# Gate pieces moved into the mixer, the first expert's matrix ahead of the ranking, modulation by token halves, and last rows and statistics ahead of the overflow test

## The chip, the core and the metric

The kernel runs on one core of a Trainium2 chip. The time is device time in microseconds (us) of one execution. Its engines are TensorE (PE; PEld is its weight load), VectorE (DVE), ScalarE (ACT), GpSimd (POOL) and SyncE (SP), which here mainly issues DMAs. Each engine works its own instructions in order and waits on semaphores for the others. All times below are in us from the start of the span unless they are durations.

## The reference

Two decoder layers on 256 tokens of 1024 channels, in float32. Each layer has two sub-layers, a token mixer and a channel mixer, and each sub-layer is modulated by the condition c:

```python
x = layer_norm(x, ln0_g, ln0_b)
for layer in range(DEPTH):
    shift, scale, gate = modulation(c, ada_w[layer, 0], ada_b[layer, 0])
    h = x * (1.0 + scale) + shift
    y = hybrid_mixer(h, ...)          # SSD, latent attention, gMLP, one output projection
    x = layer_norm(DN_ALPHA * x + (1.0 + gate) * y, ...)
    shift, scale, gate = modulation(c, ada_w[layer, 1], ada_b[layer, 1])
    h = x * (1.0 + scale) + shift
    y = swiglu(h, ...) if layer % 2 == 0 else moe_swiglu(h, ...)   # top 2 of 8 experts
    x = layer_norm(DN_ALPHA * x + (1.0 + gate) * y, ...)
```

`modulation` is silu(c) times a 1024x3072 matrix (the "ada" weights), cut into shift, scale and gate. `moe_swiglu` takes the softmax over each token's two best router logits as weights and sums the two experts' outputs.

## The kernel before, in words

The four sub-layers run one after the other: mixer 0, dense, mixer 1, experts. Weights come in chunks of 1 MB (some 0.75 MB) through a ring of buffers; SP issues the DMAs in program order, each as soon as a buffer of the ring is free.

Matmuls that need full precision are made of three (`mm3`, L153 to L155): the weight is split into a rounded part `whi` (ACT, L146) and a rest `wlo` (DVE, L148), the activation into `hhi` and `hlo`, and the products hhi·whi, hlo·whi and hhi·wlo are summed. The experts use a form of it in part, and plain float32 matmuls elsewhere.

A sub-layer starts like this. `residual` (L321, L322) adds the gated output to x, one half of 128 tokens after the other; each half gets its statistics (L285, L289), the power on POOL (L280) and its normalisation on DVE (L325, remembered as `mark["x"]`). `transposed` makes 16 transposes on PE (L332) into four PSUM tiles, each two channel blocks by 256 tokens. `modulated_t` works through these four tiles: scale and shift of one block on ACT (`htmp`, L343), of the other on DVE (L346), then the rounded part of both on ACT (`hhi`, L348), the rest on DVE (`hlo`, L349). Two `htmp` buffers are there. `proj` in the mixer (L153 to L155) and the first pieces of the dense layer then take `hhi` and `hlo` as moving operand, 256 tokens wide, channel block after channel block.

The ada pieces are 24 units of half a shift, scale or gate each: two 1 MB chunks, 16 matmuls (L200), for a gate piece the addition of a bias row on DVE (L223), a copy of the row on ACT (L225), one broadcast matmul on PE (L229, two records in the trace) and the copy into the gate on ACT (L193). `CUT` says which units fall to which stage. Units of a stage are taken from a list wherever "F" stands in `ORDER`, the written order of the steps in a mixer. Those that `CUT` leaves over (`stage[5]`, the two gate pieces of the experts' sub-layer) are worked after mixer 1, held back behind its last normalisation by `issue_after`, which tells the scheduler that an instruction must not be put ahead of another.

Routing (`route`): the normalised x is transposed and copied (`xt`, L812, L814), multiplied with the router (L818), the best two logits are found, `sl` says which expert a token goes to and `pos` at which place (L846). Then the experts are ranked by their counts (`cnt`, L864) on DVE, the ranking's tables are made, and SP loads the experts' numbers. The expert at the first place is known ahead. For each place `gather` makes a selection matrix `hot` (L933) and picks its tokens by matmul (L971, L978). Then the expert's matmuls (L1029, L1037, L1120), and `scatter` (L1165, L1169) adds the result to x. At the end, `overflow` tests whether an expert had more tokens than places (L1206), and works those off; with these inputs it has nothing to do. The last layer norm takes the statistics of x, loads its gain and bias (`lnrow`, L303, a 1 MB broadcast), and finishes four quarters of x on DVE (L1333, L1334) and on ACT with POOL (L1328 to L1330).

## Time and profile before

| | us |
|---|---|
| median of 3 runs | 1257.72 (1256.67 to 1258.25) |
| the profiled execution | 1257.42 |
| its span | 1255.6 |
| TensorE busy | 1170.9 (93%) |
| VectorE busy | 506.3 (40%) |
| ScalarE busy | 384.3 (31%) |
| read from memory | 399.61 MB, 320 GB/s over the span |

In the rows below a line begins with its start and its duration; "x8" says that eight instructions were merged in a row. What stands in square brackets is how long the engine had been idle before, and whose instruction ended the wait. PEclk is the granted clock of TensorE as a share of full speed; the levels are 2.4 GHz (1.00) and 1.2 GHz (0.50).

### The profile page before, as it was taken

The numbers are of one execution on the slowest core, as the hardware profiler recorded it, in microseconds if no ns is written. First come the engines' busy times: TensorE is split into PE (matmuls) and PEld (weight loads), VectorE is DVE, ScalarE is ACT, GpSimd is POOL, SyncE is SP. The second block draws the span as 40 slices with busy tenths as digits, with TensorE's granted clock in tenths as the row PEclk, the third lists the DMA queues.
The fourth block names the chain that finished last, engine by engine and source line by source line (L and its number), as shares of the span: only waits on it lengthen the run. The fifth ranks groups of instructions, "written<-read, shape, count | busy, mean of one in ns | idle before, by whom it ended". The sixth has DMA issues, their size and how long they took to land. (4 is left out here: it accounts for less than half of the span.)

```text
span 1255.6 us, 18705 instructions
## 1 busy us (share of the span) xinstructions
PE 1170.9 (93%) x7667; PEld 704.4 (56%) x7667; DVE 506.3 (40%) x815; ACT 384.3 (31%) x558; POOL 54.5 (4%) x58
## 2 busy tenths in 40 slices
PE   5999979999997999879999999899999999999994
PEld 2877758999986976534433557743334333333331
DVE  2776465777557754521003477630010020300214
ACT  1776435444444754210002457620010010100100
POOL 0100100000000000010000002200000000000001
PEclk9999889999998997989999999999999999999997
DMA  9957646788554475638999999999999999999994
GB/s 378 386 200 295 219 167 227 279 299 332 171 192 167 163 288 198 252 157 312 350 426 408 426 424 367 364 395 349 425 423 371 423 391 426 412 401 375 413 423 163
DMA packets 59592, 402.97 MB, mean 321 GB/s; under 512 B 6751, under 2 KB 7143, under 8 KB 17390
## 3 DMA queue, kind: packets, MB, share of 16 engines
q1 hardware_dynamic: 59358, 401.47, 81.3%
q8 instruction: 62, 1.02, 0.3%
q10 hardware_dynamic: 144, 0.26, 0.1%
q14 instruction: 28, 0.23, 0.0%
HBM read 399.61 MB, written 2.10 MB: 320 GB/s over the span
## 5 line engine op out<-in xcount | busy, mean ns | idle before, releaser
L1029 PE MATMUL mm<-w,xt 128*64 128x512 f32 (+1 forms) x1344 | 288.7, 561 | 0.0
L148 DVE TENSOR_TENSOR wlo<-w,whi 128x1024 fp32r<-128x1024 f32 (+1 forms) x180 | 220.0, 1229 | 111.9 <-ACT whi L146 110.0
L146 ACT ACTIVATE whi<-w 128x1024 fp32r<-128x1024 f32 (+1 forms) x188 | 194.1, 1041 | 177.8 <-PE mm L154 87.8
L1029 PEld LDWEIGHTS mm<-w,xt 128*64 128x64 f32 x1344 | 94.4, 137 | 165.0 <-issue 163.7
L153 PE MATMUL mm<-hhi,whi 128*128 128x256 f32 x608 | 175.5, 290 | 4.8 <-ACT hhi L348 4.8
L154 PE MATMUL mm<-hlo,whi 128*128 128x256 f32 x608 | 174.8, 288 | 0.8 <-DVE hlo L349 0.8
L155 PE MATMUL mm<-hhi,wlo 128*128 128x256 f32 x608 | 173.7, 286 | 0.0
L1072 DVE TENSOR_TENSOR sa<-mm,sa 128x512 f32<-128x512 f32 (+3 forms) x30 | 17.4, 580 | 371.9 <-PE mm L1029 193.0
L1120 PE MATMUL acc<-w,ht 128*64 128x512 f32 x616 | 146.5, 597 | 0.0
L153 PEld LDWEIGHTS mm<-hhi,whi 128*128 128x128 f32 x608 | 118.6, 195 | 9.5 <-ACT hhi L348 6.0
L154 PEld LDWEIGHTS mm<-hlo,whi 128*128 128x128 f32 x608 | 118.6, 195 | 2.4 <-DVE hlo L349 1.8
L155 PEld LDWEIGHTS mm<-hhi,wlo 128*128 128x128 f32 x608 | 118.4, 195 | 0.6 <-issue 0.5
L1120 PEld LDWEIGHTS acc<-w,ht 128*64 128x64 f32 x616 | 43.6, 137 | 81.8 <-issue 80.7
L1071 ACT ACTIVATE sa<-mm 128x512 f32<-128x512 f32 (+3 forms) x30 | 15.2, 507 | 202.6 <-PE mm L1029 116.0
L1095 ACT ACTIVATE ht<-acc 128x512 f32<-128x512 f32 (+1 forms) x21 | 11.8, 561 | 199.2 <-PE acc L1093 199.2
L1037 PE MATMUL mm<-w,xt 128*32 128x256 f32 x1056 | 70.2, 382 | 0.0
L1037 PEld LDWEIGHTS mm<-w,xt 128*32 128x32 f32 x1056 | 34.1, 109 | 44.8 <-issue 24.6
L200 PE MATMUL mm<-w,cs_rep 128*32 128x512 f32 x304 | 41.1, 654 | 9.6 <-DMA w<-in_ada_dram 9.1
L154 PE MATMUL mm<-wlo,xth 128*128 128x512 f32 (+1 forms) x96 | 36.7, 382 | 1.6 <-POOL wlo L148 1.6
L155 PE MATMUL mm<-whi,xtl 128*128 128x512 f32 (+1 forms) x96 | 36.1, 376 | 0.0
L280 POOL TENSOR_TENSOR rs<-rs,mhalf 128x1 f32<-128x1 f32 x14 | 9.1, 652 | 615.9 <-DVE rs L278 615.9
L154 PE MATMUL acc<-wlo,gh 128*128 128x512 f32 x88 | 35.1, 399 | 0.0
(331 smaller groups left out, 1337.9 us busy)
## 6 DMA issues: line engine op xcount, KB each, us to landing
w<-in_moe_dram SPq DMA_DIRECT2D x216, 1024.0 KB, 9.8
w<-in_ada_dram SPq DMA_DIRECT2D x48, 1024.0 KB, 6.7
w<-in_moe_dram SPq DMA_DIRECT2D x64, 768.0 KB, 8.4
w<-in_ffn_dram SPq DMA_DIRECT2D x33, 1024.0 KB, 4.9
w<-in_w_in_dram SPq DMA_DIRECT2D x18, 1024.0 KB, 6.5
w<-in_w_out_dram SPq DMA_DIRECT2D x8, 1024.0 KB, 8.5
lnrow<-in_lnrows_dram SPq DMA_DIRECT2D x5, 1024.0 KB, 4.9
x<-in_x_in_dram SPq DMA_DIRECT2D x2, 512.0 KB
```

The lines of the kernel that those rows point to most:

```text
L146: act.activation(hi, src, AF.Copy)
L148: eng.tensor_tensor(lo, src, f32(hi), op=OP.subtract)
L153: pe.matmul(out_ap, ah, bh, start=start, stop=False)
L154: pe.matmul(out_ap, ah, bl, start=False, stop=False)
L155: pe.matmul(out_ap, al, bh, start=False, stop=stop)
L200: pe.matmul(ps[32 * g:32 * g + 32, :], cs_rep[:, 4 * r + g, :], w[:, g, :], start=(r == 0), stop=(r == 1), tile_position=(0, 32 * g))
L1029: pe.matmul(ps[64 * c:64 * c + 64, :], st.t[:, k, 0:64], w[:, k1, half * c:half * c + half], start=(k == 0), stop=(k == KD - 1), tile_posi ...
L1037: pe.matmul(p3[32 * g:32 * g + 32, :], st.t[:, k, 64:96], w[:, k1, 256 * g:256 * g + 256], start=(k == 0), stop=(k == KD - 1), tile_positi ...
L1071: act.activation(sa[0:rows, :], src[0:rows, :], AF.Silu)
L1072: dve.tensor_tensor(sa[0:rows, :], sg[0:rows, :], sa[0:rows, :], op=OP.mult)
L1095: act.activation(ht, pt, AF.Copy)
L1120: pe.matmul(po[0][64 * c:64 * c + 64, :], th[:, t % nq, c0:c0 + 64], ws[m][:, t % 2, 512 * c:512 * c + 512], start=first(t), stop=last(t), ...
```

## The change

It has five parts. (1) `CUT` ends at 20, not 18, and `ORDER` of mixer 1 has two more "F" (after CB and after GM), so the experts' two gate pieces are worked inside mixer 1. (2) `modulated_t` goes over the two token halves, and within each over the four tiles; each instruction is half as wide, and there are twice as many. (3) The weight splits of mixer 1's projection, and of the first piece of the dense layer, are held behind `mark["x"]`. (4) The first expert's selection matrix is made in `route`, right behind `pos`. (5) The statistics of the last x are made ahead of the overflow test (and again inside it, if it has work), and `lnrow` is loaded ahead of the last expert chunks; to free its buffer, the overflow's copy of x lies in two other tiles. A branch that never ran (`EARLY`) is dropped.

```diff
-CUT = (6, 8, 13, 16, 18)
+CUT = (6, 8, 13, 16, 20)
...
-    "... GV F DEC CB Z1 QT F XDT ... F F V GM D2 W S2 ...".split(),
+    "... GV F DEC CB F Z1 QT F XDT ... F F V GM F D2 W S2 ...".split(),
...
     def modulated_t(tiles, ad):
...
-        for q in range(4):
-            tmp = wk.tile([P, 2, T], F, tag="zs", name=nm("htmp"))
-            for u in range(2):
-                k = 2 * q + u
-                if u == 0:
-                    act.activation(tmp[:, u, :], tiles[q][:, u, :], AF.Identity, bias=ad.sh[:, k:k + 1],
-                                   scale=ad.sc[:, k:k + 1])
-                else:
-                    dve.tensor_scalar(tmp[:, u, :], tiles[q][:, u, :], ad.sc[:, k:k + 1], ad.sh[:, k:k + 1],
-                                      op0=OP.mult, op1=OP.add)
-            act.activation(hhi[:, 2 * q:2 * q + 2, :], tmp, AF.Copy)
-            dve.tensor_tensor(hlo[:, 2 * q:2 * q + 2, :], tmp, f32(hhi)[:, 2 * q:2 * q + 2, :], op=OP.subtract)
+        for i in range(2):
+            ts = slice(i * P, i * P + P)
+            for q in range(4):
+                tmp = wk.tile([P, 2, P], F, tag="zs", name=nm("htmp"))
+                for u in range(2):
+                    k = 2 * q + u
+                    if u == 0:
+                        act.activation(tmp[:, u, :], tiles[q][:, u, ts], AF.Identity, bias=ad.sh[:, k:k + 1],
+                                       scale=ad.sc[:, k:k + 1])
+                    else:
+                        dve.tensor_scalar(tmp[:, u, :], tiles[q][:, u, ts], ad.sc[:, k:k + 1], ad.sh[:, k:k + 1],
+                                          op0=OP.mult, op1=OP.add)
+                ks = slice(2 * q, 2 * q + 2)
+                act.activation(hhi[:, ks, ts], tmp, AF.Copy)
+                dve.tensor_tensor(hlo[:, ks, ts], tmp, f32(hhi)[:, ks, ts], op=OP.subtract)
...
-                wh, wl = split(w[:, :, u * P:u * P + P], [P, KD, P])
+                with ExitStack() as late:
+                    if l == 1:
+                        late.enter_context(tc.issue_after(mark["x"]))
+                    wh, wl = split(w[:, :, u * P:u * P + P], [P, KD, P])
...
-                    wh, wl = split(w[:, :, u * P:u * P + P], [P, KD, P])
+                    with ExitStack() as late:
+                        if pj == 0:
+                            late.enter_context(tc.issue_after(mark["x"]))
+                        wh, wl = split(w[:, :, u * P:u * P + P], [P, KD, P])
...
         dve.tensor_copy(rs.pos, pp)
+
+        rs.hot0 = cp.tile([P, 2, P], F, name="hot0")
+        for i in range(2):
+            dve.tensor_scalar(rs.hot0[:, i, 0:CAPS[0]], iota[:, 0:CAPS[0]], rs.pos[:, i, 0:1], rs.sl[:, i, 0:1],
+                              op0=OP.is_equal, op1=OP.mult)
...
-            hot = mp.tile([P, 2, P], F, tag="hot", name=nm("hot"), bufs=2)
-            for i in range(2):
+            hot = mp.tile([P, 2, P], F, tag="hot", name=nm("hot"), bufs=2) if place else rs.hot0
+            for i in range(2) if place else ():
...
+        t = ln_chunk(4, mp, "yacc")
+        g, b = t[:, 0, :], t[:, 1, :]
         stage2(*prev)
         scatter(prev[0])
-        overflow()
-
-        t = ln_chunk(4, mp, "yacc")
-        g, b = t[:, 0, :], t[:, 1, :]
-        fin = []
-        for i in range(2):
-            st, steps = ln_stats(x[:, i, :], D)
-            for f in steps:
-                f()
-            fin.append(ln_finish(st))
+        stats = [ln_stats(x[:, i, :], D) for i in range(2)]
+
+        def moments():
+            for _, steps in stats:
+                for f in steps:
+                    f()
+
+        moments()
+        overflow(moments)
+        fin = [ln_finish(st) for st, _ in stats]
...
-    with tc.issue_after(mark["x"]):
-        for f in stage[5]:
-            f()
```

How the built programs order the work at three places (lines of the kernel after differ by a few: L147 is the split, L324 the normalisation, L347 and L351 the modulation, L199 and L228 the ada matmuls, L826 the router's matmul, L1016 an expert chunk):

VectorE at the start of mixer 1, before: the two splits (`wlo`) of the first projection piece, the second token half's normalisation of x (L325) and the first modulation steps.

```order
L148 TENSOR_TENSOR wlo_3670<-w_3666,whi_3669 128x1024
L289 BN_AGGR mv_3521<-bnst_3512 128x2
L148 TENSOR_TENSOR wlo_3698<-w_3666,whi_3697 128x1024
L278 TENSOR_SCALAR rs_3523<-mv_3521 128x1
L325 TENSOR_SCALAR x_99<-x_99,mv_3521,rs_3523 128x1024
L346 TENSOR_SCALAR htmp_3572<-acc_3545,sc_2958,sh_2959 128x256
L346 TENSOR_SCALAR htmp_3577<-acc_3546,sc_2958,sh_2959 128x256
L349 TENSOR_TENSOR hlo_3571<-htmp_3572,hhi_3570 128x512
```

The same place after.

```order
L324 TENSOR_SCALAR x_99<-x_99,mv_3561,rs_3563 128x1024
L147 TENSOR_TENSOR wlo_3657<-w_3653,whi_3656 128x1024
L347 TENSOR_SCALAR htmp_3612<-acc_3585,sc_2998,sh_2999 128x128
L347 TENSOR_SCALAR htmp_3617<-acc_3586,sc_2998,sh_2999 128x128
L147 TENSOR_TENSOR wlo_3685<-w_3653,whi_3684 128x1024
L351 TENSOR_TENSOR hlo_3611<-htmp_3612,hhi_3610 128x2x128
L351 TENSOR_TENSOR hlo_3611<-htmp_3617,hhi_3610 128x2x128
L147 TENSOR_TENSOR wlo_3730<-w_3726,whi_3729 128x1024
L347 TENSOR_SCALAR htmp_3622<-acc_3587,sc_2998,sh_2999 128x128
L347 TENSOR_SCALAR htmp_3627<-acc_3588,sc_2998,sh_2999 128x128
```

The two splits stand behind the normalisation, two more that stood ahead of this stretch come with them, and the modulation's instructions are 128 tokens wide.

TensorE in the routing, before: the last transposes of the second half, the two gate pieces (L229, L200) and the router's matmul (L818).

```order
L332 MATMUL acc_4868<-ident,x_99 128x128 x2
L332 MATMUL acc_4869<-ident,x_99 128x128 x2
L229 MATMUL mm_4904<-row_4902,sel 128x512
L200 MATMUL mm_4908<-w_4909,cs_rep 32x512 x4
L200 MATMUL mm_4908<-w_4915,cs_rep 32x512 x4
L229 MATMUL mm_4926<-row_4924,sel 128x512
L818 MATMUL mm_4938<-xt,rt 32x256 x8
```

The same place after.

```order
L331 MATMUL acc_4970<-ident,x_99 128x128 x2
L331 MATMUL acc_4971<-ident,x_99 128x128 x2
L331 MATMUL acc_4972<-ident,x_99 128x128 x2
L826 MATMUL mm_4998<-xt,rt 32x256 x8
L834 MATMUL mm_5011<-k_sb,lt_5009 128x8 x2
```

The gate pieces stand between no transposes and router any more. They stand in mixer 1 now, ahead of the gMLP's matmuls (L620 to L689):

```order
L199 MATMUL mm_4598<-w_4599,cs_rep 32x512 x4
L199 MATMUL mm_4598<-w_4605,cs_rep 32x512 x4
L228 MATMUL mm_4616<-row_4614,sel 128x512
L199 MATMUL mm_4620<-w_4621,cs_rep 32x512 x4
L199 MATMUL mm_4620<-w_4627,cs_rep 32x512 x4
L620 MATMUL mm_4639<-wkv_3606,kvn_3862 128x256 x2
L685 MATMUL mm_4643<-bs_3608,k_sb 128x256
```

The broadcast matmul L228 of a gate piece stands right behind the sums L199 of its own piece.

SP at the end of the experts, after: the last four expert chunks, `lnrow` and the overflow test (L1214).

```order
L1016 DMA w_9007<-in_moe_dram 128x2048
L302 DMA lnrow_9019<-in_lnrows_dram 128x2048
L1016 ISA
L1016 DMA w_9021<-in_moe_dram 128x2048
L1016 ISA
L1016 DMA w_9027<-in_moe_dram 128x2048
L1016 ISA
L1016 DMA w_9033<-in_moe_dram 128x2048
L1214 COMPARE_AND_BRANCH
```

Before, `lnrow` stood behind the overflow's branches, as the last load of the kernel.

## Rows read from the trace of the kernel before

**Rows 1.** The page: busy time of the engines, and the DMA share in the span's 40 slices, in tenths.

```profile
PE 1170.9 (93%) x7667; PEld 704.4 (56%) x7667; DVE 506.3 (40%) x815; ACT 384.3 (31%) x558; POOL 54.5 (4%) x58
...
DMA  9957646788554475638999999999999999999994
```

**Rows 2.** The table of stretches: the stretch, its length, busy time (and instructions) of PE, PEld, DVE, ACT and POOL, the granted clock, DMA share and GB/s.

```profile
389.20:393.20 4.00, 3.93 (x19) 3.71 (x20) 3.67 (x6) 2.89 (x6) 0.00 (x0) 0.58 0.01 2
428.00:503.00 75.00, 72.89 (x470) 51.48 (x469) 42.22 (x102) 41.92 (x77) 2.72 (x3) 0.89 0.60 225
...
478.00:491.50 13.50, 13.50 (x55) 7.11 (x55) 4.64 (x9) 5.34 (x14) 0.00 (x0) 0.50 0.45 160
...
534.00:550.20 16.20, 8.36 (x63) 4.11 (x62) 8.26 (x46) 1.79 (x4) 1.67 (x2) 0.79 0.20 86
560.00:1231.00 671.00, 655.10 (x4165) 287.68 (x4163) 156.26 (x191) 122.69 (x175) 27.60 (x18) 1.00 0.98 395
```

**Rows 3.** The timeline at the start of mixer 1: start, duration, engine, line, operation.

```profile
382.60 1.21 DVE L148 TENSOR_TENSOR wlo<-w,whi 128x1024 fp32r<-128x1024 f32 x1
...
383.85 1.17 DVE L148 TENSOR_TENSOR wlo<-w,whi 128x1024 fp32r<-128x1024 f32 x1
...
385.81 0.81 DVE L325 TENSOR_SCALAR x<-x,mv,rs 128x1024 f32<-128x1024 f32 x1 [0.73 <-POOL rs L280]
...
389.27 0.80 PE L153 MATMUL mm<-hhi,whi 128*128 128x256 f32 x2 [0.62 <-ACT hhi L348]
...
391.88 1.29 DVE L349 TENSOR_TENSOR hlo<-htmp,hhi 128x512 fp32r<-128x512 f32 x2
```

**Rows 4.** Groups of instructions by line and shape: the columns are busy time and mean ns of one, then idle time before them.

```profile
L349 DVE TENSOR_TENSOR hlo<-htmp,hhi 128x512 fp32r<-128x512 f32 x12 | 7.8, 687 | 1.0 <-ACT hhi L348 0.8
...
L346 DVE TENSOR_SCALAR htmp<-acc,sc,sh 128x256 f32<-128x256 f32 x12 | 6.2, 542 | 3.7 <-ACT htmp L343 3.4
...
L445 ACT ACTIVATE dec<-mm,nacs 128x128 f32<-128x128 f32 x16 | 6.0, 372 | 0.0
...
L409 ACT ACTIVATE xbc<-conv 128x256 f32<-128x256 f32 x12 | 4.9, 413 | 2.8 <-DVE conv L406 2.8
...
L1072 DVE TENSOR_TENSOR sa<-mm,sa 128x256 f32<-128x256 f32 x6 | 2.5, 425 | 124.8 <-PE mm L1037 124.8
...
L479 DVE TENSOR_SCALAR prob<-prob,sums 128x128 f32<-128x128 f32 x8 | 2.3, 286 | 0.2
```

**Rows 5.** The timeline at the start of the dense layer.

```profile
172.19 1.21 DVE L148 TENSOR_TENSOR wlo<-w,whi 128x1024 fp32r<-128x1024 f32 x1
...
173.43 1.17 DVE L148 TENSOR_TENSOR wlo<-w,whi 128x1024 fp32r<-128x1024 f32 x1
...
175.40 0.81 DVE L325 TENSOR_SCALAR x<-x,mv,rs 128x1024 f32<-128x1024 f32 x1 [0.73 <-POOL rs L280]
...
178.85 0.80 PE L153 MATMUL mm<-hhi,whi 128*128 128x256 f32 x2 [0.62 <-ACT hhi L348]
```

**Rows 6.** The timeline at the start of mixer 0.

```profile
30.42 1.02 ACT L343 ACTIVATE htmp<-acc,sh,sc 128x256 f32<-128x256 f32 x2 [1.82 <-DVE sh L274]
...
32.96 0.58 PE L153 MATMUL mm<-hhi,whi 128*128 128x256 f32 x1 [3.25 <-ACT hhi L348]
...
37.94 1.29 DVE L349 TENSOR_TENSOR hlo<-htmp,hhi 128x512 fp32r<-128x512 f32 x2
```

**Rows 7.** The timeline of the routing.

```profile
526.79 1.09 PE L332 MATMUL acc<-ident,x 128*128 128x128 f32 x8 [2.80 <-DVE x L325]
...
527.51 1.42 DVE L814 COPY xt<-acc 128x256 f32<-128x256 f32 x4
...
529.52 1.92 PE L200 MATMUL mm<-w,cs_rep 128*32 128x512 f32 x16
...
532.92 1.12 PE L229 MATMUL mm<-row,sel 128*128 128x512 f32 x2 [1.47 <-ACT row L225]
...
533.97 1.07 PE L818 MATMUL mm<-xt,rt 128*32 128x256 f32 x16
```

**Rows 8.** The timeline from the ranking to the first expert's gather, and (last row) the gather of the next expert.

```profile
539.44 0.17 DVE L864 COPY cnt<-mm 128x8 f32<-128x8 f32 x1 [0.20 <-PE mm L849]
...
543.34 0.32 DVE L933 TENSOR_SCALAR hot<-k_sb,pos,sl 128x96 f32<-128x96 f32 x1
...
543.42 3.26 PE L971 MATMUL acc<-x,hot 128*64 128x512 f32 x8 [4.02 <-DVE most L903]
...
573.36 1.94 PE L971 MATMUL acc<-x,hot 128*64 128x512 f32 x8
```

**Rows 9.** The timeline of the end, and the table of two stretches before it.

```profile
1231.50 0.14 PEld L1120 LDWEIGHTS acc<-w,ht 128*64 128x64 f32 x2 [0.29 <-DMA w<-in_moe_dram]
...
1240.66 1.88 DVE L285 BATCH_NORM_STATS2 bnst<-x 128x6 f32<-128x512 f32 x3 [0.25 <-DVEq L1206]
1241.35 0.35 SPq L303 DMA_DIRECT2D lnrow<-in_lnrows_dram  x1
...
1246.32 2.42 DVE L1333 SCALAR_TENSOR_TENSOR x<-x,mv,lnrow 128x512 f32<-128x512 f32 x2 [2.15 <-DMA lnrow<-in_lnrows_dram]
...
1225.00:1230.00 5.00, 5.00 (x26) 1.72 (x24) 0.00 (x0) 0.00 (x0) 0.00 (x0) 1.00 1.02 424
1230.00:1235.00 5.00, 5.00 (x24) 1.49 (x22) 0.00 (x0) 0.00 (x0) 0.00 (x0) 1.00 0.26 108
```

More of the change, by code (lines that the diff above doesn't have):

```diff
@@ L32 @@
     "P3 X0 C QP KR X1 X2 QR DT QT GV F Z0 DEC CB XDT F KVN D3 D0 KK F B0 F GU S3 V GM F S0 B1 Z1 W D2 F D1 W S2 A0 W S1 Y0 Y1 A1 F GR RMS W".split(),
-    "X0 X1 P3 C QP KR X2 QR DT Z0 KVN GV F DEC CB Z1 QT F XDT D3 KK F D0 F F GU B1 S3 S0 W B0 F F V GM D2 W S2 D1 S1 Y1 A0 W Y0 A1 GR W RMS".split(),
+    "X0 X1 P3 C QP KR X2 QR DT Z0 KVN GV F DEC CB F Z1 QT F XDT D3 KK F D0 F F GU B1 S3 S0 W B0 F F V GM F D2 W S2 D1 S1 Y1 A0 W Y0 A1 GR W RMS".split(),
 ]
@@ L39 @@
 R_CW, R_CB, R_D, R_NW, R_QN, R_KN, R_ADA, R_LN, R_END = 0, 24, 30, 34, 38, 40, 41, 89, 137
-EARLY = 2
 RANKS = [4, 0, 5, 1, 6, 2, 3]
@@ L932, in gather @@
                     slots = iota[:, None, 0:64].to_broadcast([P, 2, 64])
-                ins = (pool if place else dve).tensor_scalar(to, slots, pos[:, i, :], sl[:, i, :], op0=OP.is_equal, op1=OP.mult).ins
-                if place == 0:
-                    mark["hot"] = ins
+                pool.tensor_scalar(to, slots, pos[:, i, :], sl[:, i, :], op0=OP.is_equal, op1=OP.mult)
             st.t = mp.tile([P, KD, P], F, tag="xt", name=nm("xt"), bufs=2)
@@ L1045, in stage1 @@
                             k = 2 * j + k1
-                            with ExitStack() as late:
-                                if place == 0 and s == 0 and wsel == 0 and k >= EARLY:
-                                    late.enter_context(tc.issue_after(mark["hot"]))
-                                wh, wl = moe_split(w[:, k1, :], [P, wd])
+                            wh, wl = moe_split(w[:, k1, :], [P, wd])
                             for c in range(2):
@@ L1199, in scatter, with overflow @@
                     dve.tensor_tensor(x[:, i, :], x[:, i, :], yacc[:, i, :], op=OP.add)
-        def overflow():
+        def overflow(after):
             turn_no = mp.tile([P, 1], F, name="turn_no")
@@ L1227, in overflow @@
                         h2 = mp.tile([P, 2, P], F, tag="gtmp", name="h2")
-                        kept = mp.tile([P, 2, D], F, tag="yacc", name="kept")
-                        sp.dma_start(kept, rs.n)
+                        kept = [mp.tile([P, D], F, tag="xt", name=nm("kept"), bufs=2) for _ in range(2)]
+                        for i in range(2):
+                            sp.dma_start(kept[i], rs.n[:, i, :])
                         for i in range(2):
@@ L1236, in overflow @@
                             for i in range(2):
-                                pe.matmul(ps, kept[:, i, k * P:k * P + P], h2[:, i, :], start=(i == 0), stop=(i == 1))
+                                pe.matmul(ps, kept[i][:, k * P:k * P + P], h2[:, i, :], start=(i == 0), stop=(i == 1))
                             dve.tensor_scalar(x2[:, k, :], ps, ad.sc[:, k:k + 1], ad.sh[:, k:k + 1], op0=OP.mult, op1=OP.add)
@@ L1294, in overflow @@
                                                          op0=OP.mult, op1=OP.add)
+                after()
         gather(0)
```

## The prediction

> **What bounds the kernel now.** I read the page's shares first, then a table by stage, then the timeline at the places the change touches. TensorE is busy 93% of the span, and the DMA slices are full from the middle to the end [rows 1]. By stage [rows 2], the token mixers and the dense layer are TensorE's: in 428–503 it works 72.89 of 75 us, and nothing there waits for the weights (DMA share 0.60). The experts, 560–1231, are DMA's: share 0.98 at 395 GB/s for 671 us, with TensorE just behind. The first eleven megabyte chunks are fetched ahead and every later one waits for a buffer to be freed, so this stretch moves as a block with its first matmul. So a microsecond lost or won at any place before 550 reaches the end whole. Open time is found only where TensorE waits: three sub-layer starts, the routing (8.36 of 16.2 us busy in 534–550.2), and the last 20 us.
>
> **The token halves.** Start with mixer 1 [rows 3]. Before, two weight splits (wlo, 1.21 and 1.17 us) stand on VectorE ahead of the second half's normalisation, and the first projection matmul comes at 389.27, which is 389.27 − 385.81 − 0.81 = 2.65 us after that normalisation ends: transposes, one pair of htmp, one hhi. The change takes the two splits from before the normalisation, so it ends 2.4 us earlier. Then it puts four splits behind it, among the modulation steps.
>
> Does the first half of the tokens start before the second is normalised? In the program as built the first half's htmp still waits for the second half's transposes, since both write one PSUM tile. So it doesn't start earlier. And a projection matmul streams all 256 tokens, so it needs channel 0 of both halves, which is the fifth of eight half steps; before it needed the first of four whole ones.
>
> A half step isn't half the price. Whole: htmp 542 ns and hlo 687 ns on VectorE. The nearest half-width rows on VectorE are 286 ns (128x128) and 425 ns (128x256); on ScalarE, 372 and 413 ns [rows 4]. So until the fifth hhi, VectorE does four splits (4 × 1.22 = 4.9), four htmp and four hlo (4 × (0.33 + 0.43) = 3.0, with htmp taken between 0.29 and 0.37) and the fifth htmp 0.33, and ScalarE the hhi 0.41: 8.6 us after the normalisation, 6.0 more than 2.65. Less the 2.4, the first matmul comes 3.6 us later. The last operand follows the first matmul by some 2.6 us (three half steps of 0.8 and a hlo), where before it took 391.88 + 1.29 − 389.27 = 3.9; so the last operand is 2.3 later. Work on TensorE that could run meanwhile is the same, and half of the 24 matmuls of the first piece are still ahead at that point, so I take +3.3. Bounds: 0 (the splits hide behind the chain) to +4.5 (the slow clock, 0.58 in 389.2–393.2 [rows 2], lasts on).
>
> The dense layer starts alike: splits of 1.21 and 1.17 us, normalisation at 175.40, first matmul at 178.85 [rows 5], 2.64 us after it ends. Again +3.3, 0 to +4.5.
>
> In mixer 0 no split moves, and there is no normalisation to bring forward. Modulation took from 30.42 to 37.94 + 1.29 = 39.23, splits included, with the first matmul at 32.96 [rows 6]. After, the first four half steps keep all four splits (4.9 of those 8.8 us on VectorE), so they save at most 4 × (0.54 − 0.33 + 0.69 − 0.43) = 1.9 us, and four more half steps of about 0.8 to 1.0 us and the casts and the table load that were behind them follow: 8.8 − 1.9 + 4 = 10.9, some 2 later at the end and 6 later at the first matmul. I take the middle, +4.0; bounds +2 and +6.
>
> The Trainium skill ("Perfetto Trace Analysis", section Optimizing Scalar/DVE Operations) says that where ScalarE and VectorE aren't saturated but cause bubbles on other engines, breaking up instructions may let work complete sooner. By that rule the three starts would gain. It's the first rival below, and needs a consumer that can use a half; this one can't.
>
> **The gate pieces.** Two ada pieces leave the routing [rows 7]: each is 1.92 us of L200, a gate add, a row copy, 1.12 us of L229. Before, they stood between the second transposes and the router's matmul: from the transposes' end (526.79 + 1.09 = 527.88) to 533.97 are 6.1 us. The transposed x must still be copied (to 527.51 + 1.42 = 528.93), so the router's matmul (pq, L818) moves up by 5.0. Bounds −6.1 and −2.5: without this work TensorE is idler, and the matmuls behind may run at half clock (0.79 was granted in 534–550.2 already [rows 2]; the eight gather matmuls took 3.26 us there against 1.94 elsewhere [rows 8], and the 1.07 of pq would double).
>
> The Trainium skill ("TensorE: Matmul & The Clock Gate", section What's actually happening) says that the clock is throttled by default and released by activity; the cold gather agrees. By it, the colder routing would keep about 2.5 of the 5.0 us.
>
> In mixer 1 these pieces add 2 × (1.92 + 1.12) = 6.1 us to an engine that has 2 us of idle time in 75. In the new order the first piece's L229 stands right behind L200 of its own sums, and there it waits for VectorE and ScalarE: the same wait shows 1.47 us in the routing [rows 7]. On the other side, 13.5 us (478–491.5) ran at clock 0.50 [rows 2], and denser work before it may keep the full clock: worth up to 6. I take +6.0, the pieces themselves, as if wait and clock cancel; bounds 0 and +9. The 4 MB of weights fit: share 0.60 there.
>
> **The first expert's matrix.** Before, its two halves stood at the end of the ranking on VectorE: cnt 539.44, hot ends at 543.66, and the gather waits 4.02 us for it [rows 8]. Now they stand right behind cnt: 539.61 + 0.66 = 540.27. That is −3.4; −4.7 if the gather also warms to 1.94. Behind it on VectorE the rest of the ranking starts 0.66 later: its readers are the expert numbers for SP, which has no chunk to issue before the experts' first matmuls free a buffer, so it costs nothing; without that cover it would cost 0.66.
>
> **The end.** lnrow is issued at 1241.35, and VectorE waits 2.15 us for it, to 1246.32; the statistics start 0.25 us late, after the overflow test [rows 9]. With lnrow there both waits go: −2.4. But lnrow now stands on SP's queue ahead of the last three chunks, in a stream at share 1.02 and 424 GB/s (1225–1230) whose last chunk TensorE takes as it lands (1231.50, released by the DMA). Its 1.05 MB at 424 GB/s are 2.5 us, paid before the last matmul. Net +0.1; bounds −2.4 and +0.3.
>
> **Sum**, on the profiled execution of 1257.42 us: +4.0 + 3.3 + 3.3 − 5.0 + 6.0 − 3.4 + 0.1 = +8.3, so 1265.7. The median of the runs is 0.3 higher: 1266.0.
>
> **Rivals.** (A) Faster: the halves pay. If the first half's modulation lies beside the second's normalisation, the splits off the path bring mixer 1 and the dense start 2.4 us each and mixer 0 nothing: −4.8 in place of +10.6. With the rest (−2.3) that is −7.1: 1250.3. It decides as soon as the first matmul comes less than 2.65 us after the normalisation. For it: VectorE does free the 2.4 us. Against it: the wait and the 256 columns. Chance 0.15. (B) The modulation's delay is absorbed (TensorE has other work and catches up): starts 0, the rest −2.3: 1255.1. Against it: TensorE's waits of 2 us in 75 leave it no slack to catch up in. 0.12. (C) The ada work holds the full clock over 478–491.5, and 6.0 falls to 0: 1259.7. For it: that stretch is small matmuls without pause. Against: the clock fell there while TensorE was busy. 0.13. (D) The routing runs colder and keeps 2.5 of the gain: 1268.2. 0.15. The forecast: 0.45.
>
> **Range and chances.** From A with its point to D with the upper bounds of a start: 1251 to 1271; what is left out is part of A's lower side and the sum of several upper bounds, 0.2 together. The forecast's own range is 1261 to 1269. A change under 0.2% (2.5 us) can't be told from none. Faster: A and half of B, 0.2. Same: C and the other half of B, 0.18. Slower: 0.62.
>
> **What would show it.** In the changed profile: at mixer 1 the normalisation some 2.4 us earlier against the end of the dense layer, but the first projection matmul later, by 3.6, with four wlo between; L200 and L229 inside mixer 1's stretch and 6 us more from its first projection matmul to its last output matmul; pq within 1.5 us of the second transposes; the gather within 1 us of pos; at the end lnrow's wait gone, and the last chunk 2.5 us later against the first expert matmul. I'm wrong if the first matmul follows the normalisation by less than 4 us, or if mixer 1 is no longer by the pieces moved into it.

## The result, and the profile after

The changed kernel takes 1273.36 us (median of 4 runs, 1270.05 to 1280.32) against 1257.99; the ratio is 1.0118, with a 95% interval of 1.0081 to 1.0156. It is slower, as forecast, but by 15 us and not by 8, and 1273 lies above the range of 1251 to 1271. The profiled executions are 1257.42 and 1272.58 us, with spans of 1255.6 and 1270.7.

I took the length of each stage from the two timelines, between the same instructions:

| from, to | before | after | change | forecast |
|---|---|---|---|---|
| start to mixer 0's output projection | 137.86 | 145.79 | +7.9 | +4.0 |
| to the end of the dense layer | 238.58 | 242.08 | +3.5 | +3.3 |
| to mixer 1's output projection | 116.96 | 124.21 | +7.3 | +3.3 + 6.0 |
| to the router's matmul (pq) | 40.57 | 35.29 | −5.3 | −5.0 |
| to the first expert matmul | 16.28 | 17.29 | +1.0 | −3.4 |
| to the last expert matmul of the program | 685.35 | 688.48 | +3.1 | +2.5 |
| to the end | 19.95 | 17.60 | −2.4 | −2.4 |

Five terms came near. Two didn't: mixer 0 (3.9 too little) and the way from the router to the first expert (4.4 too much gain); mixer 1's forecast was 2.0 too high.

The timeline of the kernel after at the start of mixer 1, to be held against [rows 3]:

```profile
391.42 1.09 PE L331 MATMUL acc<-ident,x 128*128 128x128 f32 x8 [1.70 <-DVE x L324]
...
395.18 0.81 DVE L324 TENSOR_SCALAR x<-x,mv,rs 128x1024 f32<-128x1024 f32 x1 [0.73 <-POOL rs L279]
395.91 1.22 DVE L147 TENSOR_TENSOR wlo<-w,whi 128x1024 fp32r<-128x1024 f32 x1
396.05 1.97 PE L331 MATMUL acc<-ident,x 128*128 128x128 f32 x8 [3.53 <-DVE x L324]
396.78 0.94 ACT L344 ACTIVATE htmp<-acc,sh,sc 128x128 f32<-128x128 f32 x2 [2.85 <-PE acc L331]
...
401.66 1.22 DVE L147 TENSOR_TENSOR wlo<-w,whi 128x1024 fp32r<-128x1024 f32 x1
...
404.65 0.79 PE L152 MATMUL mm<-hhi,whi 128*128 128x256 f32 x2 [6.63 <-ACT hhi L350]
...
406.48 0.78 DVE L351 TENSOR_TENSOR hlo<-htmp,hhi 128x256 fp32r<-128x256 f32 x2
```

From the end of the normalisation (395.99) to the first projection matmul are 8.66 us, where the prediction had 8.6, and the last operand follows 2.6 later, as it had. TensorE waits 6.63 us in one piece for `hhi`. The first half gained nothing: its transposes ran at 391.42, but ScalarE begins its `htmp` only at 396.78, when the second half's transposes release it.

The same in mixer 0, against [rows 6]:

```profile
30.66 0.81 ACT L344 ACTIVATE htmp<-acc,sh,sc 128x128 f32<-128x128 f32 x2 [1.82 <-DVE sh L273]
...
37.62 0.81 ACT L344 ACTIVATE htmp<-acc,sh,sc 128x128 f32<-128x128 f32 x2 [0.27 <-DVE hlo L351]
...
39.88 0.79 PE L152 MATMUL mm<-hhi,whi 128*128 128x256 f32 x2 [9.93 <-ACT hhi L350]
...
40.16 1.28 ACT L537 ACT_TABLE_LOAD   x1
...
42.94 0.78 DVE L351 TENSOR_TENSOR hlo<-htmp,hhi 128x256 fp32r<-128x256 f32 x2
```

The second four half steps take 37.62 to 43.72, or 6.1 us, where I had 4: the fourth split, a row copy, three casts, a small copy and a table load stand among them. The first matmul is 6.9 us later than before, and none of that was made up.

The routing as a table of stretches: end of mixer 1 to pq, pq to the gather, gather to the first expert matmul (length, busy time of PE, PEld, DVE, ACT, POOL, then granted clock, DMA share, GB/s). First the kernel before:

```profile
519.26:533.97 14.71, 9.76 (x69) 4.74 (x67) 9.09 (x20) 2.90 (x7) 1.46 (x3) 1.00 0.72 275
533.97:543.42 9.45, 2.94 (x31) 2.13 (x30) 6.35 (x41) 0.81 (x2) 0.92 (x2) 0.78 0.35 149
543.42:550.25 6.83, 5.50 (x32) 2.01 (x33) 1.95 (x7) 0.98 (x2) 0.74 (x1) 0.80 0.00 0
```

And the kernel after:

```profile
537.94:547.37 9.43, 5.56 (x33) 4.74 (x32) 6.98 (x16) 0.98 (x4) 1.41 (x2) 0.65 0.20 86
547.37:555.71 8.34, 5.29 (x32) 3.86 (x31) 3.86 (x19) 0.55 (x3) 0.00 (x0) 0.50 0.15 64
555.71:564.66 8.95, 7.70 (x32) 2.81 (x33) 5.55 (x31) 0.98 (x2) 3.17 (x5) 0.50 0.00 0
```

The clock column is the thing to see. The clock fell to 0.65 on the way to pq and stayed at 0.50 to the first expert matmul. The same matmuls are busy 5.29 us in place of 2.94, and 7.70 in place of 5.50. The single instructions, against [rows 7, 8]:

```profile
545.47 1.97 PE L331 MATMUL acc<-ident,x 128*128 128x128 f32 x8 [1.92 <-DVE x L324]
...
547.37 1.99 PE L826 MATMUL mm<-xt,rt 128*32 128x256 f32 x16
...
555.24 0.56 DVE L858 TENSOR_SCALAR hot<-k_sb,pos,sl 128x96 f32<-128x96 f32 x2
...
555.71 3.68 PE L982 MATMUL acc<-x,hot 128*64 128x512 f32 x8 [0.59 <-DVE hot L858]
```

The selection matrix does come where the order put it, and TensorE's wait for it is 0.59 us and no longer 4.02; but the way there is slower.

### The profile page after: what moved, and what is told of

The parts are those of the page before. It is cut to its first block, busy times and chain, and to the rows that moved or that the text cites. A ratio compares the mean times of both kernels' runs of the same rounds, so it can differ in the third digit from the quotient of the medians.

```text
span 1270.7 us, 18748 instructions
## 1 busy us (share of the span) xinstructions
PE 1176.9 (93%) x7667; PEld 709.4 (56%) x7667; DVE 512.0 (40%) x839; ACT 390.4 (31%) x582; POOL 53.4 (4%) x58
## 5 line engine op out<-in xcount | busy, mean ns | idle before, releaser
L147 DVE TENSOR_TENSOR wlo<-w,whi 128x1024 fp32r<-128x1024 f32 (+1 forms) x180 | 220.4, 1231 | 105.9 <-ACT whi L145 104.7
L199 PE MATMUL mm<-w,cs_rep 128*32 128x512 f32 x304 | 41.8, 666 | 8.1 <-DMA w<-in_ada_dram 7.8
```

The source lines that it names most:

```text
L147: eng.tensor_tensor(lo, src, f32(hi), op=OP.subtract)
L199: pe.matmul(ps[32 * g:32 * g + 32, :], cs_rep[:, 4 * r + g, :], w[:, g, :], start=(r == 0), stop=(r == 1), tile_position=(0, 32 * g))
```

## Experiments

The theory after the result: the half steps are the loss, by their order; the gate pieces cost in the mixer what was forecast and were, in the routing, work that kept the clock up. The rivals: the held splits on VectorE are the loss, or the doubled instruction count is. All ratios are to the kernel before, run on the same chip; brackets are 95% intervals. Profiled executions of one instruction stream differ by some microseconds (last section), so a part is read from the single stage of a profile. A stage of one execution has its own scatter, though: mixer 1 took 116.90 us in the changed kernel's profile and 115.29 in that of the run with the last rows behind the last chunk, whose instructions are the same up to there.

**Token halves alone**, on the kernel before. The edit is the diff's `modulated_t`, and nothing else.

> The kernel before with one part alone: modulation by token halves, all first halves and then all second halves; the splits stay ahead of the normalisation. Theory 1 (each start pays for the wait on the fifth of eight half steps): mixer 0 up to its output projection 6 to 8 us longer, from the second normalisation to the end of the dense layer 204 us in place of 201, mixer 1 3 us longer: about 12 us more than before, ratio 1.009 to 1.010. Theory 2 (the loss needs the held splits too): mixer 0 alone, ratio 1.005.

Measured: 1.0101 [1.0063, 1.0138]. To mixer 0's output projection 145.09 us (137.86 before); normalisation to dense end 204.09 (201.04); normalisation to mixer 1's output projection 110.03 (107.59). That is theory 1: this part alone makes the kernel as slow as all five together.

**Whole steps in the changed kernel**: the opposite edit.

```diff
-        for i in range(2):
-            ts = slice(i * P, i * P + P)
-            for q in range(4):
+        for q in range(4):
...
```

> The changed kernel with the modulation in four whole steps of 256 tokens again; the splits stay held behind the normalisation. Theory 1 (the half steps are the loss at all three starts): mixer 0 goes back by 7 to 8 us, its first projection matmul to about 33, and the dense layer and mixer 1 by some 3 us each, since the first whole step's hhi comes about 3.5 us after the normalisation ends in place of 8.6: 1258 to 1262 us. Theory 2 (the loss in the dense layer and mixer 1 is the splits on VectorE): only mixer 0, where no split was moved, goes back: about 1265.5 us.

Measured: 0.9956 [0.9919, 0.9993], median 1256.45. To the output projection of mixer 0 138.72, the dense layer 199.94 (206.58 in the changed kernel), mixer 1 111.24 (116.90). The ratio falls by 1.6%, more than theory 1 had expected (1258 to 1262), and theory 2 is out: the dense layer and mixer 1 go back by 6.6 and 5.7 us, with the splits still held.

**Splits free in the changed kernel**: the two `issue_after(mark["x"])` of the weight splits are taken out.

> The changed kernel without the hold on the splits: the scheduler puts the four of the first piece ahead of the normalisation again; the half steps stay. Theory 1 (half steps): mixer 0 unchanged, in the dense layer and mixer 1 the normalisation 2 us later and the first matmul about 4.5 us after its end in place of 8.6; net 1 to 2 us less at each start: 1269 to 1272 us. Theory 2 (the held splits are the loss): 3.5 us less at each start, 1266 us or less.

Measured: 1.0092 [1.006, 1.0124], median 1274.6. In the dense layer the second normalisation is 2.07 us later again, and from there to the end are 204.22 in place of 206.58, so the two cancel (0.3 gained). Mixer 1 gains 1.6 (122.61 in place of 124.21 from the end of the dense layer), but that is no more than the scatter told above. The gain is nearer 0 than the 1 to 2 us per start of theory 1, and the median, 1274.6, is above its 1269 to 1272. Theory 2 is out again.

**Splits held alone**, on the kernel before: the diff's two `with ExitStack()` blocks, and nothing else.

> The kernel before with one part alone: the splits of the first pieces held behind the normalisation; modulation in whole steps. Theory 1 (two splits less ahead of the normalisation bring it 2.1 us forward, and whole steps have room for the splits): 3 us less in the dense layer from the end of mixer 0 to its own end, 3 to 5 less in mixer 1: ratio 0.994 to 0.996. Theory 2 (as forecast for the halves, the splits delay the first matmul by what the normalisation gains): ratio 0.999 to 1.001.

Measured: 0.9943 [0.9911, 0.9974], median 1253.93. The timeline of the dense start, against [rows 5]:

```profile
172.62 0.81 DVE L325 TENSOR_SCALAR x<-x,mv,rs 128x1024 f32<-128x1024 f32 x1 [0.73 <-POOL rs L280]
173.35 1.22 DVE L148 TENSOR_TENSOR wlo<-w,whi 128x1024 fp32r<-128x1024 f32 x1
...
176.07 0.80 PE L153 MATMUL mm<-hhi,whi 128*128 128x256 f32 x2 [0.62 <-ACT hhi L348]
```

2.64 us from the end of the normalisation to the first matmul, as before, though the split stands between. It lies beside the transposes and ScalarE's first `htmp`. From the end of mixer 0 to the end of the dense layer it is 3.1 us less than before. So with whole steps this part pays; I had bounded it only together with the halves. Mixer 1 is shorter too, 102.09 us from the normalisation (107.59 before), but there the clock differs as well: this profile lacks the stretch at 0.50 of [rows 2].

**Half steps, tile after tile**, in the changed kernel:

```diff
-        for i in range(2):
-            ts = slice(i * P, i * P + P)
-            for q in range(4):
+        for q in range(4):
+            for i in range(2):
+                ts = slice(i * P, i * P + P)
```

> The changed kernel with the half steps in another order: both halves of a PSUM tile behind each other, tile after tile; same instructions, same widths, same splits. Theory 1 (the order is the loss: a matmul of 256 tokens waits for the fifth of eight half steps): in mixer 0 the first matmul comes after the second half step, some 4 us sooner than in the changed kernel, and TensorE has most of its first 24 matmuls behind it when the last operand comes; 1.5 to 3 us less at each of the three starts: about 1266 us. Theory 2 (the doubled count of instructions on VectorE and ScalarE is the loss, the order is not): the last operand comes as late as in the changed kernel and the time stays within 2 us of it.

Measured: 0.9982 [0.9958, 1.0006], median 1259.85, so 13.5 us less than the changed kernel by the medians, by two exchanged loops. It can't be told from the kernel before. The first matmul of mixer 0:

```profile
34.40 0.58 PE L152 MATMUL mm<-hhi,whi 128*128 128x256 f32 x1 [4.56 <-ACT hhi L350]
```

It is at 34.40, against 39.88 in the changed kernel and 32.96 before. From the normalisation to the end of the dense layer, first the changed kernel, then this run, then whole steps (length, busy time of PE, PEld, DVE, ACT, POOL, granted clock, DMA share, GB/s):

```profile
181.29:387.87 206.58, 197.60 (x1360) 182.06 (x1364) 133.31 (x168) 91.33 (x109) 0.00 (x0) 0.96 0.66 235
174.41:375.51 201.10, 198.14 (x1360) 180.82 (x1364) 133.38 (x168) 91.13 (x109) 0.00 (x0) 0.98 0.67 241
171.24:371.18 199.94, 198.45 (x1360) 180.41 (x1364) 131.69 (x160) 89.33 (x101) 0.00 (x0) 0.98 0.67 243
```

Of the 6.6 us that the half steps cost there, 5.5 are the order and 1.2 the doubled count. Theory 1 holds, with a larger effect than the 1.5 to 3 us that it expected of each start.

**Gate pieces back in the routing**, in the changed kernel:

```diff
-CUT = (6, 8, 13, 16, 20)
+CUT = (6, 8, 13, 16, 18)
...
+    with tc.issue_after(mark["x"]):
+        for f in stage[5]:
+            f()
     rs = route(x, tiles, rt, rc)
```

(and the two added "F" of `ORDER` out)

> The changed kernel with the two gate pieces in the routing again. Theory 1 (without them the routing runs at half clock and gives most of their time back): mixer 1 4 to 6 us shorter, the router's matmul 5 us later against the end of mixer 1, but the clock stays at 1.00 up to the ranking, the gather starts 3 us sooner after the router's matmul than in the kernel before, and from gather to first expert matmul 6.8 us in place of 8.95: 1268 to 1271 us. Theory 2 (the cold routing comes from the shorter ranking, not from the gate pieces): the clock is 0.50 from the router's matmul on here too, and the time is 1273 to 1275.

Measured: 1.0069 [1.0029, 1.0109], median 1273.47 with a spread of 1264.69 to 1276.68, which can't be told from the changed kernel's. The median lies in the range of theory 2 and not in that of theory 1. The profile, of the fastest of the ten runs, shows the parts (mixer 1 from the normalisation to its output projection, then the three stretches of the routing):

```profile
394.37:502.36 107.99, 98.92 (x737) 81.37 (x737) 70.90 (x149) 66.67 (x120) 2.73 (x4) 0.93 0.57 206
...
528.23:544.06 15.83, 11.15 (x68) 5.08 (x68) 9.11 (x20) 2.90 (x7) 1.41 (x2) 0.89 0.66 253
544.06:549.98 5.92, 2.94 (x31) 2.13 (x30) 3.00 (x16) 0.81 (x2) 0.00 (x0) 1.00 0.57 241
549.98:557.12 7.14, 5.88 (x33) 1.98 (x33) 5.44 (x31) 0.98 (x2) 3.17 (x5) 0.76 0.00 0
```

In the changed kernel they are 116.90, 9.43, 8.34 and 8.95. From pq to the gather the clock is 1.00 here and 0.50 there, so on the mechanism theory 1 holds. In the routing the pieces' removal is worth 6.4 − 2.4 − 1.8 = 2.2 us and not 6.4, and in the mixer, between these two executions, they cost 8.9. The whole times don't show that net loss of 6.7: the medians are 1273.47 and 1273.36. Why the cost in the mixer can exceed the 6.1 us of matmuls that were moved is in the changed kernel's timeline of mixer 1:

```profile
488.94 1.92 PE L199 MATMUL mm<-w,cs_rep 128*32 128x512 f32 x16
493.45 2.08 PE L228 MATMUL mm<-row,sel 128*128 128x512 f32 x2 [2.58 <-ACT row L224]
495.45 3.64 PE L199 MATMUL mm<-w,cs_rep 128*32 128x512 f32 x16
```

The broadcast waits 2.58 us for the row of its own sums, and behind that wait the clock is down: the same 16 matmuls take 3.64 in place of 1.92 us.

How much the pieces cost also depends on the clock of the mixer's last part without them. With whole steps, from the normalisation to the output projection, first a run with the pieces (the filled routing below), then two without (the splits held alone, and the last run below):

```profile
380.94:492.13 111.19, 105.61 (x773) 83.32 (x773) 70.19 (x143) 66.83 (x116) 2.73 (x4) 0.94 0.63 238
379.94:482.03 102.09, 98.27 (x737) 81.89 (x737) 68.64 (x141) 64.73 (x112) 2.73 (x4) 0.96 0.60 218
379.07:486.85 107.78, 103.97 (x736) 84.34 (x736) 68.67 (x141) 64.83 (x112) 2.74 (x4) 0.90 0.57 206
```

The cost is 9.1 us where that part keeps its clock, and 3.4 where it runs at 0.50, as it did in the profile of the kernel before [rows 2].

**Filling matmuls in the routing**, on the version with whole steps, the gate pieces in the mixer, and the last rows behind the last chunk:

```diff
+    def filler(at, count):
+        with tc.issue_after(mark[at]):
+            for _ in range(count):
+                pe.matmul(mmt([P, 256]), ident, k_sb[:, 0:256], start=True, stop=True)
...
+    filler("fold", 3)
     tiles = transposed(x)
+    filler("t0", 4)
     rs = route(x, tiles, rt, rc)
```

(and `filler("pl", 3)` behind the router's second matmul)

> As the run with the whole steps, the last rows behind the last chunk, and ten matmuls of 128x256 into PSUM that nobody reads, placed in the routing's waits on TensorE (three ahead of the first transposes, four between the two halves, three behind the router's second matmul). Extra work only. Theory 1 (the routing without the gate pieces is slow because TensorE's clock falls): granted clock 1.00 from the transposes to the gather, router's matmul to gather 5.9 us in place of 7.2 to 8.3, gather to first expert matmul 6.8 to 7.2 in place of 8.95; some 3.5 us less than the run with the whole steps from the end of mixer 1 to the first expert matmul. Theory 2 (the clock isn't the reason): the same clock or not, these stretches keep their length or grow by the added matmuls' 0.5 us each where they stand in the way.

Measured: 0.9836 [0.98, 0.9872], median 1242.7. The same three stretches:

```profile
517.97:526.69 8.72, 7.00 (x48) 5.71 (x46) 6.73 (x16) 0.71 (x3) 1.41 (x2) 1.00 0.15 63
526.69:533.12 6.43, 4.87 (x36) 3.27 (x36) 3.92 (x19) 0.71 (x3) 0.00 (x0) 1.00 0.30 127
533.12:540.26 7.14, 5.87 (x32) 1.99 (x32) 5.44 (x31) 0.98 (x2) 3.19 (x5) 0.76 0.00 0
```

More work and less time: 22.3 us from mixer 1 to the first expert matmul, where the whole-steps run had 25.6 and the other profiles without pieces or filling there had 24.3 to 26.7. The clock is 1.00 up to the gather; the gather itself still takes 3.63 us. Added work can't restore an overlap, so 3.3 us of the routing's lost gain are the clock's. The medians differ by more, 1242.7 against 1256.45: in the profiles the experts are 5.3 us shorter too (685.94 against 691.24), of which the place of the last rows explains some 2 (below).

**First expert's matrix and early statistics**, on the kernel before, with the last rows loaded behind the last chunk:

```diff
+        rs.hot0 = cp.tile([P, 2, P], F, name="hot0")
...
+        moments()
+        overflow(moments)
+        t = ln_chunk(4, mp, "yacc")
```

> The kernel before with only two parts: the first expert's matrix ahead of the ranking, and statistics ahead of the overflow test with the last rows behind the last chunk. Theory 1: from the router's matmul to the gather 5.9 us in place of 9.45, the experts' stretch unchanged, the tail 2.4 us shorter: 5.5 to 6 us less than before, ratio 0.9955. Theory 2 (the experts' stretch is DMA's and takes back what is won ahead of it): the gather comes 3.4 us earlier, the last expert matmul does not; ratio 0.998.

Measured: 0.9912 [0.9878, 0.9946], median 1251.02. pq to the gather 5.92 (9.45), gather to the first expert matmul 6.92 (6.83), experts 686.35 (685.35), end 17.60 (19.95). With the gate pieces in place, the matrix is worth 3.5 us, as forecast, and the experts' stretch moves as a block. The ratio is lower than the 0.9955 expected, which lies outside the interval: the stages explain 5.9 us, and what the medians have beyond that (1251.02 against 1261.42) isn't explained.

**Last rows behind the last chunk**, in the changed kernel: `ln_chunk(4, mp, "yacc")` after `overflow(moments)`.

> The changed kernel with the last gain and bias rows loaded behind the overflow test again; the statistics stay ahead of it. Theory 1 (the megabyte ahead of the last three chunks delays them by its own time): first expert matmul to last expert matmul 2.5 to 3.1 us shorter, the tail behind it 2.2 to 2.7 us longer, the total within 0.7 us of the changed kernel. Theory 2 (the load was free in front): the experts' stretch stays, and the total grows by 2.4 us.

Measured: 1.0073 [1.0043, 1.0103]. Experts 687.28 (688.48), but the end 17.60, the same as in the changed kernel. I had missed that with early statistics nothing holds the load behind the test any more: SP issued it at 1230.87, right after the last chunk, and it landed well ahead of its use. So this experiment had no late load in it, and its expected trade didn't occur. What the load costs ahead of the chunks was still open from this pair, since the stretch scatters by 1 us.

**The parts that paid, together**: whole steps, held splits, gate pieces in the routing, early matrix, early statistics, late rows.

> The parts that paid, together: modulation in whole steps, splits held behind the normalisation, first expert's matrix ahead of the ranking, statistics ahead of the overflow test, last rows behind the last expert chunk, and the gate pieces in the routing as before. Theory 1 (gate pieces are cover in the routing that keeps the clock, and work in the mixer that costs): against the kernel before, dense start -3, mixer 1 start -2 to -3, gather -3.4, tail -2.4: ratio 0.990 to 0.992, and faster than the run with the whole steps alone. Theory 2 (moving the gate pieces pays): no faster than that run, 0.996.

Measured: 0.9899 [0.986, 0.9938], median 1250.57 (1242.17 to 1254.32). Mixer 1 102.09, to pq 15.58, to the gather 5.92. The ratio is theory 1's. That it is faster than the run with the whole steps isn't shown: the intervals overlap, and the two differ also in the place of the last rows.

**The same with three filling matmuls** behind the router's second matmul:

> The parts that paid, with the gate pieces in the routing, and three matmuls of 128x256 that nobody reads behind the router's second matmul, where TensorE waits 1.9 us for VectorE. Extra work only. Theory 1 (the gather starts at half clock because of that wait): the gather's eight matmuls take 1.9 us in place of 3.3, from gather to first expert matmul 5.5 in place of 6.9; ratio to before 0.989 or less. Theory 2 (the clock at the gather doesn't hang on that wait): 6.9 us there as without them, and the ratio 0.990.

Measured: 0.9839 [0.9803, 0.9876], median 1242.98. The two stretches, pq to gather and gather to first expert matmul, and from the timeline the gather itself:

```profile
526.97:532.90 5.93, 4.34 (x38) 3.12 (x37) 3.00 (x16) 0.81 (x2) 0.00 (x0) 1.00 0.57 239
532.90:538.54 5.64, 4.25 (x33) 1.72 (x33) 5.33 (x31) 1.08 (x3) 2.61 (x4) 1.00 0.00 0
```

```profile
532.90 1.94 PE L985 MATMUL acc<-x,hot 128*64 128x512 f32 x8 [0.50 <-DVE hot L861]
```

The gather takes 1.94 us, where it took 3.26 before [rows 8]. Both versions beat the kernel before; between this one, the run before it and the filled one above, the intervals overlap. The filled one has the gate pieces in the mixer and this one in the routing, with medians of 1242.70 and 1242.98, so by whole times their place is worth nothing that can be seen.

**The last rows ahead of the last three chunks**, on that version:

```diff
+        t = ln_chunk(4, mp, "yacc")
+        g, b = t[:, 0, :], t[:, 1, :]
         stage2(*prev)
```

> The fastest version so far (whole steps, held splits, gate pieces in the routing, three filling matmuls) with one thing put as the change has it: the last rows are loaded ahead of the last three expert chunks. Theory 1 (a megabyte ahead of them delays the last matmul by its time in the full stream): from the first to the last expert matmul 2.5 us more than the 686.6 of that version, the end behind it unchanged at 17.6: ratio to before about 0.986. Theory 2 (the stretch's length scatters by that much anyway and the load costs nothing): 686.6 within 1.0, and TensorE waits for no weights in the last 8 us.

Measured: 0.9886 [0.9859, 0.9913], median 1244.05. Experts 688.25 (686.59), end 17.59. TensorE at the end of the experts:

```profile
1220.43 1.46 PE L1131 MATMUL acc<-w,ht 128*64 128x512 f32 x6
1223.16 1.94 PE L1131 MATMUL acc<-w,ht 128*64 128x512 f32 x8 [1.27 <-DMA w<-in_moe_dram]
1225.52 1.94 PE L1131 MATMUL acc<-w,ht 128*64 128x512 f32 x8 [0.43 <-SPq L1217]
1227.96 1.94 PE L1131 MATMUL acc<-w,ht 128*64 128x512 f32 x8 [0.50 <-SPq L1217]
```

And of the same version with the rows behind the chunks:

```profile
1215.95 9.18 PE L1131 MATMUL acc<-w,ht 128*64 128x512 f32 x42
```

Here 42 matmuls run without a gap; there three waits, one for each of the last three chunks, sum to 2.2 us. Theory 1, with 1.7 us in the stretch's length (2.5 were expected) and 2.2 in waits. All profiles together say the same: the six with the load ahead of the last chunks have 688.2 to 691.9 us for the experts, the eight without 685.3 to 687.3 (mean 686.3). Three of the six, at 691.2 and more, also begin the experts at a clock of 0.92 to 0.94 over the first 20 us; the other three, 688.2 to 688.5, are 2.0 above the mean of the eight.

## Why the prediction was right and wrong

**The half steps, mechanism: right and shown.** The wait of the first half on the second half's transposes and the matmul's wait for the fifth of eight steps came as worked out. The exchanged loops show that it is the order: they keep every instruction and give 5.5 of 6.6 us back in the dense layer. The 8.6 us to the first matmul came out as well (8.66), but not by its terms, and that is luck. The sum has 4.9 for the splits, which leaves 3.7 for the steps; with the splits ahead of the normalisation, in the dense layer of the halves alone and of the run with free splits, the first matmul still comes 5.94 us after it. So the half steps cost 2.2 more than the sum had, and the splits 2.7 in place of 4.9. The rule of the first rival (the Trainium skill, "Perfetto Trace Analysis", section Optimizing Scalar/DVE Operations: breaking up instructions may let work complete sooner) found no case here: in either order the half steps took longer than whole ones, 206.58 and 201.10 against 199.94.

**Their size in the dense layer: right; in mixer 0: wrong.** The failing step is "I take the middle, +4.0; bounds +2 and +6". It measured +7.9. Two things were mis-sized in it. The second four half steps took 6.1 us and not 4, since the casts and the table load that I named as standing behind them stand among them now, and the fourth split too. And I let TensorE catch up part of the first matmul's 6 us; it made up nothing, since it ran those first matmuls at half clock until 45.8, 2 us beyond the last operand (43.72), where before it was at full clock from 38.3. Some 1.5 us of the 7.9 are scatter: over the profiles, mixer 0's output projection starts at 137.86 to 141.32 with whole steps (mean 139.9 of eight) and at 144.99 to 147.88 with halves (mean 146.2 of five), a difference of 6.4, still above the bound. The output projection behind it took 28.1 us in all five profiles with halves in this order, and 25.1 in seven of the nine others; here it was 28.1 on both sides, so the table holds none of this. Whether the halves cause it isn't shown.

**The gate pieces in mixer 1: inside the bounds, but not of one size.** The forecast +6.0 was the pieces "as if wait and clock cancel". The wait was 2.58 where I had the 1.47 of [rows 7], and the clock fell behind it. Where the last part of the mixer keeps its clock without the pieces, they cost 7.3 to 9.1 us. Where it runs at 0.50, as in the profile of before [rows 2], they cost 3.2 (122.61 with splits free against 119.40 with the halves alone, from the end of the dense layer) to 3.4. The table compares with the second kind, so the term came out 2.0 below the forecast. Rival C, that the ada work holds the clock there, stays open: none of the six profiles with the pieces in the mixer has this long stretch at 0.50, and four of the eight without have it.

**The routing: pq right, what follows wrong.** pq came 5.3 us sooner (5.0). The step that failed is "That is −3.4", the first expert's matrix. Its order worked, and alone it gives 3.5. But with the gate pieces gone TensorE's clock fell, and pq, the sums and the gather ran at 0.50. This is rival D. I had it at 2.5 us and a chance of 0.15; comparing the two profiles with the pieces in and out it is 4.2 (2.4 to the gather, 1.8 behind it). I had weighed the clock only for the 5.0 and not for the gather behind it, although the cold gather of 3.26 us was among my own rows. The Trainium skill ("TensorE: Matmul & The Clock Gate", section What's actually happening) says that activity releases the throttle; the filled routing agrees, with 1.00 where the empty one had 0.50 to 0.65.

**The end: right.** Statistics ahead of the test and no wait for the rows: 2.35 (2.4). The price of the load ahead of the last chunks: some 2 us (2.5).

**The held splits: the sign was missed.** I charged them to VectorE's way to the fifth half step. With half steps they do cost 2.7 there, about what the earlier normalisation gives (2.1). Alone, with whole steps, the part gains 3.1 us in the dense layer, since the splits fit beside the transposes. In the changed kernel the halves hide this gain.

Altogether: of the 6.8 us between the 8.3 forecast and the 15.1 by the two spans, mixer 0 is 3.9 and the way to the first expert 4.4, and mixer 1 takes 2.0 back. The halves alone cost 1.0%, as much as the whole change within its interval, so the other parts about cancel. By single stages and profiles the matrix and the early statistics gain 5.9 us (spans of 1255.6 and 1249.7), the load ahead of the last chunks loses some 2, the gate pieces lose between 1.0 (3.2 − 2.2) and 6.7 (8.9 − 2.2), and the held splits are worth nothing beside the halves. The loss by the gate pieces is seen in stages only, not in whole times.

## What to carry to other kernels

Before cutting an operation into halves, ask which piece its consumer needs first, and put the pieces in that order: the same half-wide instructions cost the dense layer 6.6 us in one loop order and 1.2 in the other. A stretch in which TensorE waits is not free to empty: look at the granted clock before and after, and if it falls, a few matmuls that nobody reads may cost less than the slow clock does. Look at what is loaded ahead of the last weights in a full DMA stream: here a megabyte there made the last matmul some 2 us later, and behind them it left the end at 17.60 as it was.

## What the runs showed of the hardware

Work that nobody reads shortened the time: ten matmuls, 1.54 + 1.89 + 1.54 = 5.0 us of TensorE, took 3.3 us off the way from mixer 1 to the first expert matmul (25.6 to 22.3).

The clock also falls behind gaps of under 1 us, in some executions and not in others. The last two runs have the same instructions but for the place of one load at the end. In the later part of mixer 1, first the one with the rows behind the chunks, then the one with the rows ahead:

```profile
465.00:473.00 8.00, 7.07 (x58) 4.26 (x57) 6.95 (x28) 7.90 (x21) 0.00 (x0) 1.00 0.65 213
473.00:481.00 8.00, 7.91 (x51) 4.84 (x51) 3.80 (x12) 3.25 (x9) 0.00 (x0) 1.00 0.96 344
```

```profile
466.30:474.30 8.00, 7.03 (x48) 4.16 (x48) 4.59 (x22) 4.38 (x16) 0.00 (x0) 0.93 0.76 271
474.30:482.30 8.00, 8.00 (x32) 3.87 (x32) 2.19 (x4) 2.72 (x7) 0.00 (x0) 0.50 0.54 207
```

In the first rows of both TensorE is busy alike, with the same two waits of 0.30 and 0.72 us; behind them the one stays at 1.00 and the other goes to 0.50, busy all the time. From the normalisation to the output projection that is 102.05 against 107.78 us. Mixer 0's output projection has two lengths in the same way, 25.1 and 28.1, in kernels that are alike there (28.08 before, 25.13 with the early matrix). What decides it wasn't found. It goes with the spread of the runs: of the kernel before, the run of 1256.80 us had a mean clock of 0.973, that of 1270.45 one of 0.961. That is the reason why gains of under 3 us were read from single stages.
